# A hybrid decoder layer on one core: which engine makes four low parts of weights, the order of the state-space output, and where a query block is loaded

## The chip, the core and the metric

The kernel runs on one core of a Trainium2 chip. Its engines each run their own instructions in a fixed order: TensorE (PE in the profile) multiplies matrices, VectorE (DVE), ScalarE (ACT) and GpSimd (POOL) work elementwise, SyncE (SP) issues DMAs, and ScalarE and GpSimd issue some too. An instruction waits on its engine until what it reads is there and what it overwrites is free, and everything behind it on that engine waits as well. The metric is the time of one execution on the device, in microseconds (us). Three executions of the kernel before took 1641.96, 1643.04 and 1648.83 us; the median is 1643.04.

## The reference

The layer takes 512 tokens of width 1024 with 16 learned ones ahead, in float32. Two branches are merged by gates, and a mixer of experts follows.

```python
xn = rmsnorm(h, norm1_g[l])
proj = xn @ w_in[l]
u_s, x_m, z_m, g_s, g_m = jnp.split(proj, splits, axis=-1)     # 512, 1024, 1024, 1024, 1024 columns
y_s = s5_branch(u_s, ...) @ w_ssm_out[l]        # state-space scan, gelu, y * sigmoid(y @ w_glu + b_glu)
y_m = mlstm_branch(x_m, z_m, ...) @ w_ml_out[l] # causal convolution, 4 heads, matrix memory, gates
mixed = jax.nn.sigmoid(g_s) * y_s + jax.nn.sigmoid(g_m) * y_m
h = h + mixed @ w_out[l]
h = h + peer_ffn(rmsnorm(h, norm2_g[l]), peer_w_q[l], peer_sub_keys[l], peer_u[l], peer_v[l])
```

`peer_ffn` makes queries (`xb @ w_q`, 8 heads of 256 columns), picks 16 of 16384 experts per head by product keys, and sums the chosen rows of a table V, weighted by gates and by the gelu of products with rows of a table U.

## The kernel before

**Products in three parts.** A float32 product is made of three fast matmuls: each operand is cut into a high part (rounded to the type fp32r) and a low part (what the rounding left), and high x high, high x low and low x high are added up in one result buffer. In the profile these are L87, L90 and L91 (`mm3`) or L290, L292 and L293 (`proj`). `row3` is `mm3` with its matmuls kept in the order of the program; everywhere else a scheduler puts each engine's instructions in an order by its own estimates, before the kernel runs. `later(a, b)` adds a wait by hand: `a` comes after `b`.

**Blocks of weights.** `wblock` (L166) serves all weights of the front: a DMA on SP brings a block of 128 x 1024 into a raw buffer (`wraw`, two of them in turn), ScalarE copies it to the high part (L173, names ending in `_h`), and VectorE or GpSimd subtracts to make the low part (L176, recorded at L195, names ending in `_l`). High and low parts have two buffers each as well. `nblk` counts the blocks: 1 to 4 are those of u, then come wx0 (5), wgs0 (6), wx1 (7), wgs1 (8), wx2 (9), wgs2 (10) and so on, up to 24 for the second block of w_glu (`wglu2`), four blocks of w_ssm_out (25 to 28) and all later ones. L176 sends the low parts of blocks 2, 3, 6, 8 and of all from 29 on to GpSimd, the others to VectorE. The trace drops numbers from names: wx_l is the low part of any wx block.

**The stages that matter here.**
- *Projections.* PE multiplies xn (`xnh`, `xnl`) by the blocks of u, x (results `xm`, 264 columns at a time) and g_s (results `gs`). VectorE takes the results out (`xmt`, `mix`) and in the same time prepares the state-space scan: powers of the transition (`pw_r`, `pw_i`), and large products for its matrices (`w1r`, `w1i` and the helper `t`, in the listings `t3`, made from `s5p`; 128 x 2048 each). GpSimd does little besides.
- *State-space output* (L776 to L806). The scan's output `yg` is gated and split into `y2h` and `y2l`, four pieces (L775). Then y2 is multiplied by w_ssm_out: eight outputs so0 to so7, each of 4 x 3 matmuls of 512 columns, with two outputs to a block (wso0, wso2, wso4, wso6). Each sits in one of the four buffers of pool `mm` until VectorE multiplies it into `mix`. For the first two outputs the program writes piece 3 of y2 last.
- *Output and queries* (L1093 to L1150). `mixed` is multiplied by w_out in two passes over column halves, `c` = 0 and 1. In the second pass, for each of four tiles of 128 tokens, VectorE adds the output to x (`x0`, `x12`, `x3q`), ScalarE sums its squares (L1132), a chain of ten small VectorE steps takes the root (`n2e` is its first), L1142 scales, and PE transposes the result (`x2t`, L1108). Then the first two query blocks wq0 and wq1 are used; the other 14 follow in the expert stage.
- *Expert stage* (from about 450 us to the end): PE multiplies by the tables U (results `h`) and V (results `o`) block by block.

**Memory.** `half(name, slot)` names a tile in a fixed slot; a new tile of a slot waits until the old one has been read for the last time. Slot pB0 holds low parts of w_out in the first pass and later the tile `xn3`, of which only the half `xn3[:, 0]` is used (the scaled third tile).

Of the kernel before, what the change touches and what calls it, by code (L numbers as in the profile page):

```python
# [18 lines left out]
OP = mybir.AluOpType  # L19
# [4 lines left out]
P = 128  # L24
D = 1024
NK = D // P
# [36 lines left out]
def f32(ap):  # L63
    return ap.bitcast(F32)
# [68 lines left out]
def front(tc, a, dbg, cst, dram, xnp, ident, h2d, xsd, gds, x0, qt01, dump, split, mm3, rsqrt, rsqrt_cols):  # L133
    nc = tc.nc
    V, A, PE, GP, SY = nc.vector, nc.scalar, nc.tensor, nc.gpsimd, nc.sync
    es = ExitStack()
    with es:
# [7 lines left out]
        nblk = [0]  # L145
        NG = 20

        def half(name, slot, shape=(P, 4, T), dt=F32):

            pool = phase["pool"] if slot[0] == "p" else lng  # L150
            return pool.tile(list(shape), dt, tag=slot, name=name)
# [7 lines left out]
        highs, parts = [], {}  # L159
# [6 lines left out]
        def wblock(src, name, nk=NK, raw=None, on=None):  # L166

            if raw is None:
                raw = wload(src, name, nk)
            hi = wp.tile([P, NK, P], F32R, tag="whi", name=f"{name}_h")  # L170
            lo = wp.tile([P, NK, P], F32R, tag="wlo", name=f"{name}_l")
            nblk[0] += 1
            h_ = A.activation(hi[:, :nk], raw[:, :nk], AF.Copy)  # L173
            if on is not None:
                highs.append(later(h_, on))
            i_ = tt(lo[:, :nk], raw[:, :nk], f32(hi[:, :nk]), OP.subtract, GP if nblk[0] in (2, 3, 6, 8) or nblk[0] > NG + 8 else V)  # L176
            parts[name] = h_, i_
            if nblk[0] > NG + 22 and blank:
                blanks.append(later(SY.dma_start(blank.pop(0), zero.unsqueeze(1).to_broadcast([P, 2, D])), i_))
            return hi, lo  # L180

        def later(ins, on):

            tc.add_manual_dep(ins.ins, on.ins.name, mybir.DependencyInfo(
                mybir.DependencyClass.Sync, mybir.DependencyReason.SCHED_ONLY), reason="order")
            return ins
# [7 lines left out]
        def tt(o, x, y, op, eng=V):  # L194
            return eng.tensor_tensor(o, x, y, op=op)  # L195
# [180 lines left out]
        for j in range(L):  # L376
            for o, x in ((pv_r, pw_r), (pv_i, pw_i)):
                i_ = A.copy(o[:, :, j], x[:, :, L - 1 - j])
# [209 lines left out]
        for t_ in range(L):  # L588

            n = CH * (t_ + 1)  # L590
# [127 lines left out]
        def row3(ps_, lh, ll, rh, rl, first, last):  # L718
            row.matmul(ps_, lh, rh, start=first, stop=False)
            row.matmul(ps_, lh, rl, start=False, stop=False)  # L720
            return row.matmul(ps_, ll, rh, start=False, stop=last)
# [44 lines left out]
        for b in range(4):  # L766
            if b == 2:
                wb2 = wblock(a["w_glu"][b:b + 2].rearrange("b p k n -> p b k n"), f"wglu{b}")
            hi, lo = (x[:, b % 2 * 4:b % 2 * 4 + 4] for x in wb2)
            p = ptr(f"glu{b}")  # L770
            proj(hi, lo, p, lambda k: [ygh[:, k], ygl[:, k]], 4)
            sg = half(f"sglu{b}", ("pBr", "pBi")[b % 2], (P, S))
            A.activation(sg, p, AF.Sigmoid, bias=bglu[:, b:b + 1])
            tt(yg[:, b], yg[:, b], sg, OP.mult)
            lo_ = split(y2h[:, b], y2l[:, b], yg[:, b])  # L775
        dump("ys_glu", yg)  # L776
        sos = []

# [3 lines left out]

        for b in range(NK):
            if b % 2 == 0:
                wb2 = wblock(a["w_ssm_out"][b:b + 2].rearrange("b p k n -> p b k n"), f"wso{b}")
            hi, lo = (x[:, b % 2 * 4:b % 2 * 4 + 4] for x in wb2)
            p = pmm(f"so{b}", (P, L, NCR))
            sos.append((p, hi, lo, range(3) if b < 2 else range(4)))
            if b == 0:
                continue  # L790
            for p, hi, lo, ks in sos + [(*x[:3], (3,)) for x in sos if b == 1]:
                for k in ks:
                    mm3(p, hi[:, k], lo[:, k], y2h[:, k], y2l[:, k], k == 0, k == 3)
            done = [(n, sos[n][0]) for n in range(2)] if b == 1 else [(b, p)]
            sos = []
            for b_, p in done:
                opened_(b_, p)
# [6 lines left out]
        crs = half("crs", "pCi")[:H]  # L804
        for i in range(NT):
            cr = crs[:, i]  # L806
            V.tensor_scalar(dv[:, :i + 1], dv[:, :i + 1], fl[:, ST[i + 1] - 1:ST[i + 1]], None, op0=OP.add)
            V.tensor_scalar(cr[:, :NM], li[:, :NM], dv[:, 0:1], None, op0=OP.add)
            sh = [H, i + 1, P]
            tt(cr[:, NM:NM + (i + 1) * P].rearrange("h (j s) -> h j s", s=P),  # L810
               li[:, NM:NM + (i + 1) * P].rearrange("h (j s) -> h j s", s=P),
               dv[:, 1:i + 2].unsqueeze(2).to_broadcast(sh), OP.add)
            row.matmul(cbp[32 * i:32 * i + 32, 10], cr[:, :32], ident[:H, :H], start=True, stop=True)
            for j in range(i + 1):
                row.transpose(cbp[:, slot(j, i)], cr[:, NM + j * P:NM + (j + 1) * P], ident[:H, :H])
            row.transpose(cbp[:, 14 + i], em[:, NM + i * P:NM + (i + 1) * P], ident[:H, :H])
# [276 lines left out]
        for c, slots in ((0, ("pA1", "pB0", "mix0", "xmt0")), (1, ("xct0", "xct1", "pA0", "pB1"))):  # L1093
            wo = wout(c, slots)
            if c == 1:
                g2 = wp.tile([P, D], F32, tag="wraw", name="g2", bufs=2)
                A.dma_start(g2, a["g2"].to_broadcast([P, D]))
                xh = [xnp.tile([P, 4, S], F32R, tag="xn", name=f"x2h{j}") for j in range(2)]
                xl = [xnp.tile([P, 4, S], F32R, tag="xn", name=f"x2l{j}") for j in range(2)]
                wq = [wblock(a["w_q"][s_], f"wq{s_}") for s_ in range(2)]  # L1100
                qp = []
            def turned_(i, xn):

                first = None
                for j in range(2):
                    p = ptr(f"x2t{i}{j}", (P, 4, P))
                    for k in range(4):
                        i_ = PE.transpose(p[:, k], xn[:, (4 * j + k) * P:(4 * j + k + 1) * P], ident)  # L1108
                        if i > 1 and not first:
                            tc.keep_in_program_order(i_)  # L1110
                        first = first or i_
                    low[0] = split(xh[j][:, :, i * P:(i + 1) * P], xl[j][:, :, i * P:(i + 1) * P], p)

            def query(s_, n):

                t = slice(n * S // 2, (n + 1) * S // 2)
                if n == 0:
                    qp.append(pmm(f"q{s_}"))
                proj(*wq[s_], qp[s_][:, t], lambda k: [x[k // 4][:, k % 4, t] for x in (xh, xl)])
                A.copy(qt01[:, s_, t], qp[s_][:, t])  # L1120

            waiting = []
            for i in range(NT):
                p = pmm(f"wo{i}{c}")
                for k in range(NK):
                    lh, ll = (x[k // 4][:, k % 4, i * P:(i + 1) * P] for x in (mxh, mxl))
                    mm3(p, lh, ll, *wo[k], k == 0, k == NK - 1)
                cc = slice(c * 512, (c + 1) * 512)
                tt(xs[i][:, cc], p, xs[i][:, cc], OP.add)
                if c == 0:  # L1130
                    ss2.append(sm.tile([P, 2], F32, name=f"ss2{i}"))
                A.activation(sqj[:, cc], xs[i][:, cc], AF.Square, scale=1.0 / math.sqrt(D), accum_out=ss2[i][:, c:c + 1])  # L1132
                if c == 0:
                    continue
                A.dma_start(h2d[i * P:(i + 1) * P], xs[i])

                rstd = rsqrt_cols(sm, ss2[i][:, 0:1], 1, "n2", more=ss2[i][:, 1:2],
                                  pin=(lambda i_: later(i_, low[0])) if i == 2 else lambda i_: i_)
                if i == 1:
                    xn12, xn3 = half("xn12", "pA1", (P, 2, D)), half("xn3", "pB0", (P, 2, D))  # L1140
                xn = (xn12[:, 0], xn12[:, 1], xn3[:, 0])[i - 1] if i else x0
                V.scalar_tensor_tensor(xn, xs[i], rstd, g2, op0=OP.mult, op1=OP.mult)  # L1142
                if i == NT - 1:
                    A.dma_start(xsd, xn[P - MS:])
                waiting.append((i, xn))
                if i < 2:
                    turned_(*waiting.pop())
            if c:
                for s_ in range(2):
                    query(s_, 0)  # L1150
                    turned_(*waiting.pop(0))
                for s_ in range(2):
                    query(s_, 1)
# [800 lines left out]
```

## Time and profile before

| | us |
|---|---|
| median of three executions | 1643.04 |
| the profiled execution's own time | 1645.03 |
| its span, from the first to the last instruction | 1643.3 |
| busy: PE | 1612.1 |
| busy: VectorE | 1340.0 |
| busy: ScalarE | 727.8 |
| busy: GpSimd | 701.2 |

The mean granted clock of PE is 0.995 of full speed. In the timeline a row gives the start and the length of an instruction in us, its engine, line, operation and tiles, its shape, and in brackets how long the engine stood idle ahead of it and what ended that. Matmuls overlap: the step from start to start is what one costs PE, not its length. In a row of a window come the window's length, then busy time and number of instructions of PE, its weight loads, VectorE, ScalarE and GpSimd, then the granted clock, the busy share of the DMA engines and GB/s.

### The profile page before, as it was taken

The page shows a single profiled execution, that of the slowest core. Times are in us where ns is not written, and L with a number is a line of the kernel's source. Part 1 is how long each engine was busy: PE and PEld are TensorE (multiplying, and loading weights), DVE is VectorE, ACT ScalarE, POOL GpSimd, SP SyncE. Part 2 cuts the span into 40 slices and gives each one's busy share as a digit, 9 for nine tenths or more (in the row PEclk, how much of TensorE's full clock was granted, in tenths as well). Part 3 has the DMA queues.
Part 4 walks back from the last instruction along what each step waited for, and adds up shares of the span by engine and source line. Part 5 has one row for each costly group of instructions (what it writes and reads, how often), then busy time and mean ns, then how long its engine had stood idle before and what let it go on. Part 6 is the DMA issues. An engine that isn't in the chain of part 4 may idle for free. (4 is left out here: it accounts for less than half of the span.)

```text
span 1643.3 us, 25970 instructions
## 1 busy us (share of the span) xinstructions
PE 1612.1 (98%) x9671; PEld 1438.8 (88%) x9671; DVE 1340.0 (82%) x2675; ACT 727.8 (44%) x1202; POOL 701.2 (43%) x481
## 2 busy tenths in 40 slices
PE   9899999999999999999999999999999999999997
PEld 8798878888789899999999888888888888888886
DVE  6997556566578899999896498988988889898987
ACT  4454646733333244575664543334334333333334
POOL 3100023233122576877866244444444455555630
PEclk9999999999999999999999999999999999999999
DMA  4513322136463256889999899999999999999973
GB/s 170 117 53 95 112 81 73 60 106 216 153 221 99 74 138 175 271 294 344 304 363 319 325 373 393 385 373 367 399 372 399 357 398 382 371 401 366 389 282 139
DMA packets 148728, 423.48 MB, mean 258 GB/s; under 512 B 38485, under 2 KB 57557, under 8 KB 139129
## 3 DMA queue, kind: packets, MB, share of 16 engines
q1 hardware_dynamic: 87096, 263.52, 44.7%
q0 software_dynamic: 55360, 151.07, 26.0%
q10 hardware_dynamic: 6144, 7.23, 1.4%
q8 instruction: 76, 1.25, 0.3%
q14 instruction: 52, 0.42, 0.1%
HBM read 376.39 MB, written 45.38 MB: 257 GB/s over the span
## 5 line engine op out<-in xcount | busy, mean ns | idle before, releaser
L87 PE MATMUL h<-x2h,uh 128*128 128x352 f32 x1024 | 333.4, 326 | 1.5 <-ACT act L1239 0.9
L91 PE MATMUL h<-x2h,ul 128*128 128x352 f32 x1024 | 331.3, 324 | 3.0 <-DVE ul L84 2.9
L90 PE MATMUL h<-x2l,uh 128*128 128x352 f32 x1024 | 330.9, 323 | 0.0
L1276 POOL DMA_INDIRECT g<-in_v,e x128 | 187.6, 1466 | 160.3 <-DVE ac L1291 138.3
L87 PE MATMUL o<-vh,wh 128*128 128x512 f32 x768 | 240.5, 391 | 1.6 <-ACT wh L1820 1.6
L83 ACT ACTIVATE uh<-u 128x1024 fp32r<-128x1024 f32 x128 | 134.9, 1060 | 239.2 <-PE h L90 217.5
L90 PE MATMUL o<-vl,wh 128*128 128x512 f32 x768 | 240.0, 390 | 0.1
L1276 POOL DMA_INDIRECT g<-in_u,e x120 | 140.8, 1173 | 208.0 <-DVE g L1283 180.1
L91 PE MATMUL o<-vh,wl 128*128 128x512 f32 x768 | 224.0, 390 | 0.0
L1559 POOL DMA_INDIRECT gds<-cw,ix x96 | 189.3, 1972 | 57.0 <-DMA gds<-cw,ix 29.7
L87 PEld LDWEIGHTS h<-x2h,uh 128*128 128x128 f32 x1024 | 193.1, 189 | 6.8 <-ACT act L1239 2.5
L91 PEld LDWEIGHTS h<-x2h,ul 128*128 128x128 f32 x1024 | 192.4, 188 | 5.8 <-DVE ul L84 4.0
L90 PEld LDWEIGHTS h<-x2l,uh 128*128 128x128 f32 x1024 | 192.5, 188 | 1.8
L83 ACT ACTIVATE vh<-v 128x1024 fp32r<-128x1024 f32 x128 | 135.2, 1057 | 125.1 <-PE o L91 105.5
L84 DVE TENSOR_TENSOR vl<-v,vh 128x1024 fp32r<-128x1024 f32 x128 | 156.0, 1219 | 33.9 <-ACT vh L83 33.6
L84 DVE TENSOR_TENSOR ul<-u,uh 128x1024 fp32r<-128x1024 f32 x128 | 155.2, 1216 | 28.5 <-ACT uh L83 28.3
L91 PEld LDWEIGHTS o<-vh,wl 128*128 128x128 f32 x768 | 143.9, 188 | 30.3 <-DVE wl L1836 0.3
L90 PEld LDWEIGHTS o<-vl,wh 128*128 128x128 f32 x768 | 143.8, 188 | 29.4 <-DVE vl L84 0.4
L87 PEld LDWEIGHTS o<-vh,wh 128*128 128x128 f32 x768 | 143.2, 188 | 29.5 <-ACT wh L1820 2.3
L1291 DVE SCALAR_TENSOR_TENSOR ac<-g,w,ac 128x1024 f32<-128x1024 f32 x127 | 162.5, 1279 | 0.8
L1283 DVE SCALAR_TENSOR_TENSOR g<-g,x 128x1024 f32<-128x1024 f32 x120 | 144.5, 1216 | 0.0
L1820 ACT ACTIVATE wh<-w 128x384 fp32r<-128x384 f32 x128 | 66.9, 522 | 121.0 <-DVE w L1806 119.9
(579 smaller groups left out, 3125.4 us busy)
## 6 DMA issues: line engine op xcount, KB each, us to landing
u<-in_ut SPq DMA_DIRECT2D x64, 1024.0 KB, 7.7
v<-in_v SPq DMA_DIRECT2D x128, 512.0 KB, 9.0
gd<-stg SPq DMA_DIRECT2D x9, 2048.0 KB, 9.0
gi<-gd SPq DMA_DIRECT2D x16, 1152.0 KB, 16.1
ad<-act SPq DMA_DIRECT2D x38, 352.0 KB, 5.0
act<-ad SPq DMA_DIRECT2D x38, 352.0 KB, 11.4
wq<-in_w_q SPq DMA_DIRECT2D x14, 512.0 KB, 3.6
gds<-qt SPq DMA_DIRECT2D x6, 1024.0 KB, 5.3
```

The source lines that it names most:

```text
L83: pin(A.activation(hi, src, AF.Copy))
L84: return eng.tensor_tensor(lo, src, f32(hi), op=OP.subtract)
L87: i_ = PE.matmul(ps, lh, rh, start=first, stop=False)
L90: PE.matmul(ps, lh, rl, start=False, stop=False)
L91: return PE.matmul(ps, ll, rh, start=False, stop=last)
L1276: return GP.indirect_dma_start(out=t, out_offset=None, in_=a["u"] if s_ < P else a["v"], in_offset=bass.IndirectOffsetOnAxis(ap=e0[:, c:c ...
L1283: i_ = V.scalar_tensor_tensor(g, g, 1.0, x0, op0=OP.mult, op1=OP.mult, accum_out=hsl[:, c:c + 1])
L1291: i_ = V.scalar_tensor_tensor(ac0, g, w0[:, c:c + 1], ac0, op0=OP.mult, op1=OP.add)
L1559: i_ = GP.indirect_dma_start(out=gds.rearrange("i g b j t -> (i g b j t)").unsqueeze(1), out_offset=bass.IndirectOffsetOnAxis(ap=ix[:, c:c ...
L1820: tc.keep_in_program_order(A.activation(wh, w, AF.Copy))
```

## The change

```diff
@@ wblock
-            i_ = tt(lo[:, :nk], raw[:, :nk], f32(hi[:, :nk]), OP.subtract, GP if nblk[0] in (2, 3, 6, 8) or nblk[0] > NG + 8 else V)
+            i_ = tt(lo[:, :nk], raw[:, :nk], f32(hi[:, :nk]), OP.subtract, GP if nblk[0] in (2, 3) or nblk[0] > NG + 8 and name[:2] != "wq" else V)
@@ state-space output
-            lo_ = split(y2h[:, b], y2l[:, b], yg[:, b])
+            lo_ = split(y2h[:, b], y2l[:, b], yg[:, b], pin=halved.append)
...
-                wb2 = wblock(a["w_ssm_out"][b:b + 2].rearrange("b p k n -> p b k n"), f"wso{b}")
+                wb2 = wblock(a["w_ssm_out"][b:b + 2].rearrange("b p k n -> p b k n"), f"wso{b}",
+                             on=halved[-1] if b == 2 else None)
             hi, lo = (x[:, b % 2 * 4:b % 2 * 4 + 4] for x in wb2)
             p = pmm(f"so{b}", (P, L, NCR))
-            sos.append((p, hi, lo, range(3) if b < 2 else range(4)))
+            sos.append((p, hi, lo))
             if b == 0:
                 continue
-            for p, hi, lo, ks in sos + [(*x[:3], (3,)) for x in sos if b == 1]:
-                for k in ks:
-                    mm3(p, hi[:, k], lo[:, k], y2h[:, k], y2l[:, k], k == 0, k == 3)
+            for ks in ((0, 1), (2,), (3,)) if b == 1 else (range(4),):
+                for p, hi, lo in sos:
+                    for k in ks:
+                        row3(p, hi[:, k], lo[:, k], y2h[:, k], y2l[:, k], k == 0, k == 3)
...
-            V.tensor_scalar(dv[:, :i + 1], dv[:, :i + 1], fl[:, ST[i + 1] - 1:ST[i + 1]], None, op0=OP.add)
+            i_ = V.tensor_scalar(dv[:, :i + 1], dv[:, :i + 1], fl[:, ST[i + 1] - 1:ST[i + 1]], None, op0=OP.add)
+            if i == 0:
+                later(i_, parts["wso2"][1])
@@ queries
-                wq = [wblock(a["w_q"][s_], f"wq{s_}") for s_ in range(2)]
+                xn3 = half("xn3", "pB0", (P, 2, D))
+                raw = xn3[:, 1].rearrange("p (k n) -> p k n", k=NK)
+                SY.dma_start(raw, a["w_q"][1])
+                wq = [wblock(a["w_q"][s_], f"wq{s_}", raw=(None, raw)[s_]) for s_ in range(2)]
...
-                    xn12, xn3 = half("xn12", "pA1", (P, 2, D)), half("xn3", "pB0", (P, 2, D))
+                    xn12 = half("xn12", "pA1", (P, 2, D))
```

The low parts of wgs0 (block 6) and wgs1 (block 8), and of wq0 and wq1, go from GpSimd to VectorE. The matmuls of the state-space output go by `row3`: pieces 0 and 1 of y2 for so0 and so1, then piece 2, then piece 3, then each later output by itself. The high part of wso2 waits for the high part of y2's last piece, and the first step of the `crs` chain on VectorE waits for wso2's low part. The raw data of wq1 is loaded into the unused half `xn3[:, 1]`, so its DMA waits for slot pB0 and not for a `wraw` buffer.

The scheduler then orders the engines anew. In VectorE's order for the projections, around the low part of wx2 (numbers behind the names are the program's own), this stood before:

```order
L195 TENSOR_TENSOR w1r_581<-s5p_114 128x2048
L195 TENSOR_TENSOR xmt0_602<-xm11_732,nt_355 128x264
L195 TENSOR_TENSOR t3_585<-s5p_114 128x2048
L195 TENSOR_TENSOR w1i_582<-s5p_114 128x2048
L195 TENSOR_TENSOR wx2_l_931<-wx2_w_928,wx2_h_930 128x1024
L195 TENSOR_TENSOR w1r_581<-w1r_581,t3_585 128x2048
L195 TENSOR_TENSOR mix0_601<-gs1_815,nt_355 128x512
L195 TENSOR_TENSOR wgs2_l_992<-wgs2_w_989,wgs2_h_991 128x1024
```

and this stands there now:

```order
L195 TENSOR_TENSOR wx2_l_931<-wx2_w_928,wx2_h_930 128x1024
L195 TENSOR_TENSOR w1r_581<-s5p_114 128x2048
L195 TENSOR_TENSOR t3_585<-s5p_114 128x2048
L195 TENSOR_TENSOR w1i_582<-s5p_114 128x2048
L195 TENSOR_TENSOR mix0_601<-gs1_815,nt_355 128x512
L195 TENSOR_TENSOR wgs2_l_992<-wgs2_w_989,wgs2_h_991 128x1024
L195 TENSOR_TENSOR xmt0_602<-xm20_934,nt_355 128x264
L195 TENSOR_TENSOR w1r_581<-w1r_581,t3_585 128x2048
```

The low part of wx2 has moved ahead of three products of 128 x 2048, and the second step of w1r behind the low part of wgs2.

On PE, in the middle of the first four outputs of the state-space branch, the order before was:

```order
L87 MATMUL so0_2078<-y2h_1992,wso0_h_2074 128x512
L87 MATMUL so1_2079<-y2h_1992,wso0_h_2074 128x512
L87 MATMUL so2_2112<-y2h_1992,wso2_h_2108 128x512
L87 MATMUL so3_2126<-y2h_1992,wso2_h_2108 128x512
L90 MATMUL so0_2078<-y2l_1993,wso0_h_2074 128x512
L91 MATMUL so0_2078<-y2h_1992,wso0_l_2075 128x512
L90 MATMUL so1_2079<-y2l_1993,wso0_h_2074 128x512
L91 MATMUL so1_2079<-y2h_1992,wso0_l_2075 128x512
L90 MATMUL so2_2112<-y2l_1993,wso2_h_2108 128x512
L91 MATMUL so2_2112<-y2h_1992,wso2_l_2109 128x512
L90 MATMUL so3_2126<-y2l_1993,wso2_h_2108 128x512
L91 MATMUL so3_2126<-y2h_1992,wso2_l_2109 128x512
```

Now the last pieces of so0 and so1 stand by themselves, and so2 begins behind them:

```order
L711 MATMUL so0_2078<-y2h_1992,wso0_h_2074 128x512
L711 MATMUL so0_2078<-y2l_1993,wso0_h_2074 128x512
L711 MATMUL so0_2078<-y2h_1992,wso0_l_2075 128x512
L711 MATMUL so1_2079<-y2h_1992,wso0_h_2074 128x512
L711 MATMUL so1_2079<-y2l_1993,wso0_h_2074 128x512
L711 MATMUL so1_2079<-y2h_1992,wso0_l_2075 128x512
L711 MATMUL so2_2112<-y2h_1992,wso2_h_2108 128x512
L711 MATMUL so2_2112<-y2l_1993,wso2_h_2108 128x512
L711 MATMUL so2_2112<-y2h_1992,wso2_l_2109 128x512
```

Before, the four outputs end one right behind the other; now so0 and so1 end 24 matmuls ahead of so3 (the rows are recorded at L711, the helper of `row3`).

On ScalarE, at the end of the second output pass, the squares of token tiles 2, 3 and 0 (L1132) and the high parts of the query blocks stood like this:

```order
L1132 ACTIVATE x3q_4086,ss22_4193<-x12_4085 128x512
L173 ACTIVATE wq0_h_4251<-wq0_w_4249 128x1024
L1132 ACTIVATE x3q_4086,ss23_4221<-x3q_4086 128x512
L173 ACTIVATE wq1_h_4257<-wq1_w_4255 128x1024
L1132 ACTIVATE x3q_4086,ss20_4137<-x0_68 128x512
```

and now, with the square at L1139 of the changed file:

```order
L1139 ACTIVATE x3q_4086,ss22_4193<-x12_4085 128x512
L173 ACTIVATE wq0_h_4253<-wq0_w_4251 128x1024
L173 ACTIVATE wq1_h_4257<-xn3_4249 128x1024
L1139 ACTIVATE x3q_4086,ss23_4221<-x3q_4086 128x512
L1139 ACTIVATE x3q_4086,ss20_4137<-x0_68 128x512
```

The high part of wq1, read from xn3, has moved ahead of the square of the last tile of the first pass; the square of tile 0 in the second pass stays behind both.

## The prediction

> **What bounds the kernel now.** I read the engine shares first, then busy time by stretch, then what the matrix engine (PE) waits for.
>
> ```profile
> PE 1612.1 (98%) x9671; PEld 1438.8 (88%) x9671; DVE 1340.0 (82%) x2675; ACT 727.8 (44%) x1202; POOL 701.2 (43%) x481
> ...
> 40.00:153.40 113.40, 108.59 (x989) 101.06 (x989) 106.89 (x159) 53.80 (x95) 5.87 (x4) 0.98 0.32 80
> ...
> 1000.00:1200.00 200.00, 200.00 (x976) 174.08 (x975) 172.45 (x267) 74.98 (x133) 86.68 (x74) 1.00 1.00 383
> ...
> PE xm L293 <- DVE wx_l L195: 3.3, 2, 2.7
> PE x2t L1108 <- DVE x L1142: 2.2, 1, 2.2
> ...
> PE gs L87 <- ACT wgs_h L173: 0.9, 1, 0.9
> ```
>
> PE is the bound: it is idle for 31 us in all. In a stretch of the expert stage (1000 to 1200) it has no idle time at all. So a microsecond saved before that stage moves everything behind it, and the change can win only what PE loses in the three places it touches: the projections (40 to 153 us, where VectorE too is busy for 106.89 of 113.40 us), the state-space output (200 to 224) and the queries (around 440). The three wait rows (sum, times, longest) put 6.4 us there. That is not all, because a long wait also leaves PE at half clock:
>
> ```profile
> 54.36 0.39 PE L293 MATMUL xm<-xnh,wx_l 128*128 128x264 f32 x1 [0.68 <-DVE wx_l L195]
> ...
> 65.33 0.39 PE L290 MATMUL xm<-xnh,wx_h 128*128 128x264 f32 x1
> ...
> 66.99 0.50 PE L87 MATMUL gs<-xnh,wgs_h 128*128 128x512 f32 x1 [0.91 <-ACT wgs_h L173]
> ...
> 70.38 0.39 PE L293 MATMUL xm<-xnh,wx_l 128*128 128x264 f32 x1 [2.66 <-DVE wx_l L195]
> ...
> 70.87 0.42 PE L293 MATMUL xm<-xnh,wx_l 128*128 128x264 f32 x1
> ...
> 74.32 0.28 PE L290 MATMUL xm<-xnh,wx_h 128*128 128x264 f32 x1
> 74.44 0.29 PE L292 MATMUL xm<-xnl,wx_h 128*128 128x264 f32 x1
> ...
> 70.90:74.10 3.20, 3.20 (x16) 3.20 (x16) 3.20 (x3) 0.63 (x1) 0.00 (x0) 0.50 0.50 164
> ```
>
> Behind the 2.66 us wait the granted clock (the first number after the engines) is 0.50. From 70.87 to 74.32 sixteen matmuls start, 0.22 us apart; from 74.32 on they are 0.12 apart. That is 3.45 - 16 x 0.12 = 1.5 us lost after the wait. [...]
>
> **Part 1, the projections.** The change moves the low parts of the first two gate blocks (blocks 6 and 8) from GpSimd (POOL) to VectorE, and the scheduler then orders VectorE anew.
>
> ```profile
> 42.69 1.99 DVE L84 TENSOR_TENSOR wqkl<-wqk,wqkh 128x32 fp32r<-128x32 f32 x1
> ...
> 56.16 0.20 DVE L195 TENSOR_TENSOR ptmp<-pw_i,pw_r 128x32 f32<-128x32 f32 x1
> ...
> 57.67 1.82 DVE L195 TENSOR_TENSOR pw_i<-pw_i,ptmp 128x32 f32<-128x32 f32 x1
> ...
> 64.71 2.28 DVE L195 TENSOR_TENSOR t<-s5p 128x2048 f32<-128x2048 f32 x1
> ...
> 69.11 1.22 DVE L195 TENSOR_TENSOR wx_l<-wx_w,wx_h 128x1024 fp32r<-128x1024 f32 x1
> 70.24 2.28 DVE L195 TENSOR_TENSOR w1r<-w1r,t 128x2048 f32<-128x2048 f32 x1
> 72.45 0.68 DVE L195 TENSOR_TENSOR mix<-gs,nt 128x512 f32<-128x512 f32 x1
> ...
> 42.24 2.39 POOL L195 TENSOR_TENSOR wgs_l<-wgs_w,wgs_h 128x1024 fp32r<-128x1024 f32 x1 [3.71 <-ACT wgs_h L173]
> 57.03 2.41 POOL L195 TENSOR_TENSOR wgs_l<-wgs_w,wgs_h 128x1024 fp32r<-128x1024 f32 x1 [12.40 <-ACT wgs_h L173]
> ```
>
> Two tiny VectorE operations take 1.99 and 1.82 us, and both end within 0.1 us of a POOL operation's end (42.24 + 2.39 and 57.03 + 2.41). I take it that POOL held VectorE up. A row of their size takes 0.20 (56.16), so 1.8 + 1.6 = 3.4 us go. The two low parts come in at 1.13 us each (69.11 to 70.24, start to start), 2.3 in all. VectorE gains 1.1 us although it gets more work.
>
> The order matters more. Before, the low part of wx2 stands behind w1r, t and w1i, rows of 2.2 us each (64.71 to 69.11 for the last two), and ends at 70.24. After, it stands ahead of them. The same work, with both moved parts, ends at 70.24 - 1.1 = 69.1, so wx2's low part is ready at 69.1 - 6.6 = 62.5. PE, which starts on wx2 at 65.33, asks for it at about 65. So the 0.91 wait (a gate matmul that only stood there as a filler), the 2.66 wait and its 1.5 us of half clock go. The 0.68 wait goes too: the low part of wx1 ends some 1.3 us earlier, the 1.1 above less what is still to come from POOL's second operation, plus four short rows now behind it. Together **0.68 + 0.91 + 2.66 + 1.5 = 5.8 us**.
>
> What is late next? PE ends wx2's 48 matmuls at 65.33 - 0.68 + 48 x 0.12 = 70.4 and asks for the low part of the next gate block two gate matmuls of 0.227 (below) later, at 70.9. On VectorE it stands behind w1i and the product mix (0.68): 69.1 + 0.7 + 1.1 = 70.9. There is no margin. Later PE must not overtake VectorE:
>
> ```profile
> 152.65 0.71 DVE L195 TENSOR_TENSOR xct<-xct,qt 128x528 f32<-128x528 f32 x1 [0.71 <-ACT qt L493]
> ...
> 160.00 0.43 PE L647 MATMUL gate<-xct,wgt 128*32 128x264 f32 x4
> ...
> 153.61 4.60 ACTq L634 DMA_DIRECT2D yd<-ys  x4
> ```
>
> The gates need the last convolved block, which is 160.00 - 153.36 = 6.6 us early. After, PE is 5.8 earlier and VectorE 1.1, which leaves 1.9. The DMAs at 153.61 follow VectorE too, and so does what waits for them. For such places I take 0.8 us off: part 1 saves 5.0, with 1.0 (below) and 5.8 as ends.
>
> **Part 2, the state-space output.**
>
> ```profile
> 199.92 0.39 PE L87 MATMUL so<-y2h,wso_h 128*128 128x512 f32 x1
> ...
> 204.00 0.39 PE L87 MATMUL so<-y2h,wso_h 128*128 128x512 f32 x1
> ...
> 224.42 0.22 PE L711 MATMUL cbp<-ident,crs 4*32 4x4 f32 x2
> ...
> 204.31 0.63 ACT L83 ACTIVATE y2h<-yg 128x512 fp32r<-128x512 f32 x1 [1.69 <-DVE yg L195]
> ...
> 209.64 4.33 DVE L195 TENSOR_TENSOR mix<-so,mix 128x512 f32<-128x512 f32 x4 [2.90 <-PE so L91]
> ...
> 209.86 2.02 ACT L173 ACTIVATE wso_h<-wso_w 128x1024 fp32r<-128x1024 f32 x2 [4.92 <-PE so L90]
> ```
>
> 96 matmuls take 24.5 us. The first 18 start 0.227 apart (199.92 to 204.00); at that step all need 21.8. The 2.7 us come from an order in which the first four outputs all end together: then four products of VectorE (4.33 us) and two splits of weights come at once, and the next four outputs wait for result buffers and low parts. In the fixed order outputs 0 and 1 end after 24 matmuls, at about 205.4, and each product (1.1) has 12 matmuls, 2.7 us, beside it. The added wait holds the second block's split until the last y2 split is out (204.31 + 0.63 = 204.9 in before; earlier without that weight split ahead of it), and high and low part take 1.0 and 1.2 more, so both are ready within a microsecond of PE's asking, from 205.4 on. Behind it on ScalarE stand only the splits of blocks 4 and 6, which wait for PE anyway; the 4-row chain held behind it on VectorE is short and wanted at 221.8. **2.7 us**, with 1.5 (a low part 1.2 us late) as the low end.
>
> **Part 3, the queries.**
>
> ```profile
> 428.55 0.68 DVE L195 TENSOR_TENSOR x<-wo,x 128x512 f32<-128x512 f32 x1
> ...
> 428.66 7.42 SPq L163 DMA_DIRECT2D wq_w<-in_w_q  x2
> ...
> 440.92 1.90 DVE L110 SCALAR_TENSOR_TENSOR n2e<-ss 128x1 f32<-128x1 f32 x1 [6.23 <-ACT x3q L1132]
> ...
> 439.22 1.06 ACT L173 ACTIVATE wq_h<-wq_w 128x1024 fp32r<-128x1024 f32 x1 [5.41 <-DMA wq_w<-in_w_q]
> 440.41 2.40 POOL L195 TENSOR_TENSOR wq_l<-wq_w,wq_h 128x1024 fp32r<-128x1024 f32 x1 [4.69 <-ACT wq_h L173]
> ...
> 445.94 1.69 PE L1108 MATMUL x2t<-ident,x 128*128 128x128 f32 x8 [2.23 <-DVE x L1142]
> ...
> 453.08 1.03 PE L1108 MATMUL x2t<-ident,xn 128*128 128x128 f32 x8
> ...
> 446.40:449.50 3.10, 3.10 (x11) 2.68 (x10) 1.90 (x12) 1.69 (x4) 0.00 (x0) 0.50 0.42 169
> ```
>
> The sum of squares that the transposes need stood on ScalarE behind wq's second split, and that behind a DMA which waited for a raw buffer (the issue row of 7.42 us). With half of xn3 as its buffer that load goes out right behind the first. The second load of before took 3.1 (436.08 to 439.22); two in line land at 428.7 + 6.2 = 434.9, and the split ends at 436.0. VectorE does the low part (1.1) and x (0.7); then come the square (0.6, 440.28 to 440.92), n2e without POOL (0.2 as at 56.16, for 1.90) and the rest of the root and the scaling (3.1, from 442.82 to PE's start at 445.94). That makes 441.7. PE comes at 445.94 - 2.23 = 443.7, so 2 us of cover. The 2.23 wait goes, with its half clock: 1.69 - 1.03 on the transposes and 1.2 on six output matmuls in the 0.50 window. **4.1 us**; low end 0.
>
> **Sum.** 5.0 + 2.7 + 4.1 = 11.8, say 12. The profiled execution took 1645.03, so 1633.0 there; it stands 2.0 over the median of 1643.04, which gives **1631.0**.
>
> **Rivals.**
> - *VectorE stays the bound of the projections.* For it: 106.89 of 113.40 us busy. [...] In rows: if the 1.99 and 1.82 were no hold-up, VectorE is 3.4 later, PE waits 3.3 for the next gate block and loses 1.5 to the clock. Part 1 then saves about 1.0, all three 7.8: 1635.2. Against it: both long rows end where POOL's do.
> - *The second query load doesn't go out early*, because its half tile shares slot pB0 with weights of the first output pass. Part 3 saves nothing: 1635.1. Against: those weights are read for the last time ahead of the 428.55 row, which adds that pass's last output.
> - *The gain is swallowed later*, DMA being busy for 1.00 of 1000 to 1200: 1643. Against: PE waits for no DMA there.
> - *Slower: moved pieces in the expert stage.* The new order shifts a dozen blocks among PE's later matmuls by up to some 80 places. A piece that now comes before its low part costs a wait and the half clock, 2.23 + 1.9 = 4.1 us as above. From the third such place the gain is gone; five cost 20.5 and give 1651.5. Against: in most of that stage PE waits for nothing.
>
> **How the numbers follow.** Forecast 0.62, with a range of its own from 1628 to 1634; VectorE the bound 0.15; load not early 0.08; swallowed 0.10; slower 0.05. The range 1627 to 1638 takes in the first three, which is 0.85, less some for error. A measurement of this kernel can tell about 0.5% (8.2 us) from no change: faster means under 1634.8. That is the forecast and a third of the next two, about 0.68; slower 0.04; the rest the same.
>
> **What would show it.** Right: no half-clock window near 71 and 446; VectorE's longest 128x32 rows about 0.2; so's 96 matmuls in under 22.3 us; ScalarE's second wq split ending near 436 on this time scale less about 8. Wrong: a wait of over 2 us for a gate block's low part near 71, a transposes' wait still there, or PE idle beyond 700 us grown by as much as the front has saved.

## The result, and the profile after

| | before | changed |
|---|---|---|
| median of the first six runs each, us | 1644.02 | 1636.26 |
| lowest and highest | 1641.96 to 1648.83 | 1634.53 to 1637.24 |
| the profiled execution's own time | 1645.03 | 1634.53 |
| its span | 1643.3 | 1632.4 |

The ratio is 0.9949, with a 95% interval from 0.9934 to 0.9963; nine further runs of the changed kernel gave 0.9957 (0.9943 to 0.9970). The change saves 7.8 us, where 12 were forecast. That is 0.5%, small but clear of the noise, as both intervals end below 1. The forecast of 1631.0 is missed by 5.3 us: 4.2 are the smaller saving, 1.0 the median of before, which is 1644.02 in six runs where three had given 1643.04.

First the line of busy times of the changed kernel, then its two longest waits of PE between 40 and 160 us (sum, times, longest).

```profile
PE 1608.0 (99%) x9671; PEld 1438.1 (88%) x9671; DVE 1338.6 (82%) x2679; ACT 726.6 (45%) x1202; POOL 702.0 (43%) x477
...
PE xm L290 <- DVE mix L195: 2.2, 1, 2.2
PE gs L91 <- DVE wgs_l L195: 0.6, 1, 0.6
```

The waits that were forecast to go have gone: those for wx_l, wgs_h, so and x2t are no longer in the list. In their place stands one of 2.2 us on VectorE's product `mix`. The timeline of VectorE and ScalarE shows how it came:

```profile
42.89 0.18 DVE L84 TENSOR_TENSOR wqkl<-wqk,wqkh 128x32 fp32r<-128x32 f32 x1
...
59.76 0.19 DVE L195 TENSOR_TENSOR pw_i<-pw_i,ptmp 128x32 f32<-128x32 f32 x1
...
62.56 1.23 DVE L195 TENSOR_TENSOR wx_l<-wx_w,wx_h 128x1024 fp32r<-128x1024 f32 x1 [0.47 <-ACT wx_h L173]
65.82 2.29 DVE L195 TENSOR_TENSOR w1r<-s5p 128x2048 f32<-128x2048 f32 x1 [2.04 <-ACT s5p L378]
68.03 2.28 DVE L195 TENSOR_TENSOR t<-s5p 128x2048 f32<-128x2048 f32 x1
70.23 2.29 DVE L195 TENSOR_TENSOR w1i<-s5p 128x2048 f32<-128x2048 f32 x1
72.43 0.69 DVE L195 TENSOR_TENSOR mix<-gs,nt 128x512 f32<-128x512 f32 x1
73.03 1.22 DVE L195 TENSOR_TENSOR wgs_l<-wgs_w,wgs_h 128x1024 fp32r<-128x1024 f32 x1
...
61.47 1.06 ACT L173 ACTIVATE wx_h<-wx_w 128x1024 fp32r<-128x1024 f32 x1 [0.51 <-DMA wx_w<-in_w_in]
62.43 0.34 ACT L378 COPY s5p<-pw_i 128x16 f32<-128x16 f32 x2
62.67 0.83 ACT L484 ACTIVATE xct<-xmt,par 128x528 f32<-128x528 f32 x1
63.50 1.28 ACT L537 ACT_TABLE_LOAD   x1
64.80 0.63 ACT L537 ACTIVATE mix<-mix 128x512 f32<-128x512 f32 x1
65.33 0.46 ACT L378 COPY s5p<-pw_r 128x16 f32<-128x16 f32 x3
```

The two VectorE operations that took 1.99 and 1.82 us now take 0.18 and 0.19: GpSimd did hold them up (a later run puts two such operations back and shows the hold-up again). The low part of wx2 ends at 63.79, in time. But then VectorE stands idle for 2.04 us, until ScalarE's copies of the powers (`s5p`, L378) are made, and these stand behind a table load of 1.28 and the first gate's sigmoid of 0.63. `w1r`, `t`, `w1i`, the product of gate 1 and the low part of wgs2 follow one another without a gap, all late by that. PE's rows and three windows (engines as before, then the granted clock):

```profile
73.27 0.36 PE L290 MATMUL xm<-xnh,wx_h 128*128 128x264 f32 x1 [2.21 <-DVE mix L195]
...
74.31 0.55 PE L91 MATMUL gs<-xnh,wgs_l 128*128 128x512 f32 x1 [0.56 <-DVE wgs_l L195]
74.65 0.63 PE L87 MATMUL gs<-xnh,wgs_h 128*128 128x512 f32 x1
...
78.06 0.40 PE L91 MATMUL gs<-xnh,wgs_l 128*128 128x512 f32 x1
...
74.70:78.00 3.30, 3.30 (x9) 2.63 (x8) 3.30 (x3) 0.83 (x1) 0.00 (x0) 0.50 0.54 156
431.00:440.00 9.00, 9.00 (x45) 7.55 (x44) 6.64 (x25) 2.08 (x7) 0.00 (x0) 1.00 0.29 117
1000.00:1200.00 200.00, 200.00 (x978) 174.24 (x977) 171.33 (x264) 76.42 (x135) 85.70 (x74) 1.00 0.99 378
```

PE loses 2.21 + 0.56 us, and then eight matmuls take 3.41 us (74.65 to 78.06) where 8 x 0.227 = 1.8 would do: 1.6 more at half clock. Around the transposes (431 to 440) PE is busy throughout at full clock.

For the other two parts, the first rows are PE's at the start and behind the end of the 96 matmuls of the state-space output (219.81 - 197.96 = 21.85 us), the last two ScalarE's split of the second query block and the first step of the root:

```profile
197.96 0.39 PE L711 MATMUL so<-y2h,wso_h 128*128 128x512 f32 x1
...
219.81 0.22 PE L711 MATMUL cbp<-ident,crs 4*32 4x4 f32 x2
...
428.62 1.06 ACT L173 ACTIVATE wq_h<-xn 128x1024 fp32r<-128x1024 f32 x1 [0.18 <-DMA xn<-in_w_q]
...
432.88 0.16 DVE L110 SCALAR_TENSOR_TENSOR n2e<-ss 128x1 f32<-128x1 f32 x1 [0.79 <-ACT x3q L1139]
```

The split ends at 429.68. The end of the state-space output came 4.6 us earlier than before, so this is 434.3 on the scale of the profile before, where 436 had been forecast; and the root's first step takes 0.16 us where it took 1.90.

Executions differ by some 3 us in when the first xm matmul starts (39.39 to 42.77), so stages are measured within one trace: **P** from the first xm matmul to the first gate matmul, **S** from the first so matmul to the first cbp matmul, **Q** from there to the first matmul of the key scores (`sc`), **E** from the first gather matmul (`gp`) to the last matmul of the expert stage. For the kernel before P is 160.00 - 40.92, S is 224.42 - 199.92. The runs are told of below; each was set against runs of the kernel before on the same chip.

| kernel | P | S | Q | E | median (runs) |
|---|---|---|---|---|---|
| before | 119.08 | 24.50 | 246.79 | 955.57 | 1644.02 (6) |
| before, second profile | 119.65 | 24.54 | 245.25 | 954.39 | |
| changed | 116.85 | 21.85 | 242.64 | 953.34 | 1636.26 (6) |
| changed, second profile | 117.33 | 21.86 | 242.71 | 954.69 | 1636.24 (9) |
| part 1 alone | 117.02 | 24.54 | 246.74 | 956.15 | 1639.53 (10) |
| part 2 alone | 119.23 | 21.85 | 244.77 | 954.03 | 1640.91 (10) |
| part 3 alone | 119.12 | 24.53 | 242.71 | 954.71 | 1642.24 (10) |
| copies first | 113.56 | 21.85 | 242.71 | 957.82 | 1634.49 (6) |
| copies and low part first | 112.30 | 21.86 | 242.74 | 957.86 | 1633.90 (6) |
| the same, second profile | 112.37 | 21.86 | 242.70 | 954.60 | 1634.07 (6) |

### The profile page after: what moved, and what is told of

Read it like the earlier page. It is cut to its first block, busy times and chain, and to the rows that moved or that the text cites. A ratio compares the mean times of both kernels' runs of the same rounds, so it can differ in the third digit from the quotient of the medians.

```text
span 1632.4 us, 25970 instructions
## 1 busy us (share of the span) xinstructions
PE 1608.0 (99%) x9671; PEld 1438.1 (88%) x9671; DVE 1338.6 (82%) x2679; ACT 726.6 (45%) x1202; POOL 702.0 (43%) x477
## 4 chain that ended last, share of the span: by engine, by line
PE 85%; DVE 8%; DMA 3%; ACT 2%; issue 1%; POOL 0%; ACTq 0%; SPq 0%; DVEq 0%
PE o L87 10%; PE o L90 10%; PE o L91 10%; PE h L91 9%; PE h L87 9%; PE h L90 8%; PE gm L711 3%; PE z L711 2%; PE gp L1646 2%; PE so L711 1%; PE q L90 1%; PE q L87 1%; PE q L91 1%; PE n L711 1%; PE wo L87 1%
## 5 line engine op out<-in xcount | busy, mean ns | idle before, releaser
L1283 POOL DMA_INDIRECT g<-in_v,e x128 | 197.9, 1546 | 149.3 <-DVE ac L1298 124.8
L87 PE MATMUL o<-vh,wh 128*128 128x512 f32 x768 | 244.9, 391 | 1.5 <-ACT wh L1827 1.5
L90 PE MATMUL o<-vl,wh 128*128 128x512 f32 x768 | 244.3, 390 | 0.1
```

The costliest lines, as they stand in the source:

```text
L87: i_ = PE.matmul(ps, lh, rh, start=first, stop=False)
L90: PE.matmul(ps, lh, rl, start=False, stop=False)
L1283: return GP.indirect_dma_start(out=t, out_offset=None, in_=a["u"] if s_ < P else a["v"], in_offset=bass.IndirectOffsetOnAxis(ap=e0[:, c:c ...
```

## The experiments

**The changed kernel again, and each part alone.** No edit for the first; the other three take one part of the diff and leave the other two out.

> The changed kernel once more, as a measure of what two profiles of one kernel differ by. Theory (the 2.2 us that the changed kernel's profile gains behind 650 us, at a wait of 1.64 us at 798 that shrank to 0.35 and at short gate matmuls at 910, are a matter of one execution): the waits of the front come again within 0.1 us (2.2 near 73, the gates at 158.0, the cb matmuls at 219.8, the last query matmul at 454.9), but the wait near 788 is over 1 us again, and the span is about 1633.5 to 1635. Rival (they come from the new order of matmuls in the expert stage): the wait near 788 stays under 0.5 us and the span stays within 0.5 us of 1632.4.

> The change's first part alone: the low parts of the first two gate blocks on VectorE, all else as before. Theory (the three parts are independent; this one wins only 2.2 of the 5.0 us that were forecast, since a wait of 2.2 us and a stretch at half clock come back near 73): the gate matmuls that began at 160.00 begin at 158.0, the state-space output takes 24.5 us as before, the transposes still wait 2.2 us, and the time is 2.2 us below that of before. Rival (the new wait near 73 comes from the other two parts' orders): no wait of over 1 us near 73, and the gates at about 155.5.

> The change's second part alone: the state-space output in fixed order with its two waits, low parts and queries as before. Theory (independent parts): the front up to 199.92 as before, the 96 matmuls in 21.8 us, the matmuls behind them 2.65 us earlier than before, and that is kept to the end of the front: time 2.7 us below before. Rival (the earlier y2 splits and waits shift work of the projections too): the gates move from 160.00 by more than 0.3 us.

> The change's third part alone: the second query block loaded into half of xn3, both low parts of queries on VectorE. Theory (independent parts): nothing moves up to 440; the transposes' wait of 2.2 us and the half clock behind it go, and the last query matmul of the front comes 4.1 us earlier; time 4.1 us below before. Rival (the expert stage gives part of it back, since its DMAs are the bound there): 4.1 us earlier at 465, less than 3 at 1600.

The stages answer in the table. Part 1 moves P alone, from 119.1 to 117.0, with the new wait in it; part 2 moves S alone among P and S, by 2.65; part 3 alone brings Q to 242.71, 4.1 less than in the first profile of before. So the parts are independent, and the new wait belongs to part 1. In ratios, part 1 has 0.9975 (0.9963 to 0.9988), part 2 0.9982 (0.9968 to 0.9995), part 3 0.9992 (0.9980 to 1.0005): 4.1, 3.0 and 1.3 us of 1643.68. The first is more than P gives, the last less than Q gives, and its interval takes in no change at all. Single executions of one kernel lie 3 to 8 us apart, and a part's worth is read from its stage, not from these.

One surprise stands in Q: part 2 alone has 244.77, though it leaves the queries as they were. The changed kernel's second profile decides on the expert stage: E is 954.69 where it was 953.34, with a wait of 1.7 us near 788 that was 0.2 in the first. So most of the 2.2 us that the first profile gained there were a matter of that execution, though its span of 1632.7 is nearer to what the rival had named; the second profile of before, with 954.39, shows none of them.

**The kernel before, a second profile.**

> The kernel before once more, for a second profile. Theory (the waits come from the order and recur in every execution, the half clock behind them does not: behind the wait of 24.5 it came in three of five profiles so far): waits of 2.66 near 70 and 2.2 near 446 again, within 0.5 us; stretches at half clock behind them may be missing, and where one is missing the time behind it is 1.5 to 1.9 us less. Rival (the half clock follows from the wait's length): a half-clock stretch of over 3 us behind both waits again, as in the first profile.

This is one execution, of 1644.80 us. The wait near 70 recurred to the hundredth, 2.66, with half clock behind it (0.50 in the first window below). At the transposes the wait was 1.69, and the clock stayed at 1.00:

```profile
72.23 0.59 PE L293 MATMUL xm<-xnh,wx_l 128*128 128x264 f32 x1 [2.66 <-DVE wx_l L195]
...
447.90 1.09 PE L1108 MATMUL x2t<-ident,x 128*128 128x128 f32 x8 [1.69 <-DVE x L1142]
...
72.40:75.80 3.40, 3.40 (x16) 3.40 (x17) 3.40 (x3) 0.63 (x1) 0.00 (x0) 0.50 0.51 154
...
448.10:450.10 2.00, 2.00 (x14) 1.78 (x13) 1.01 (x6) 1.56 (x4) 0.00 (x0) 1.00 0.36 145
```

So Q of the old queries is 246.79, 245.25, 246.74 and 244.77 in four profiles, 245.9 in the mean, and with part 3 it is 242.7 every time. Part 3 is worth 3.2 us in the mean: some 4.1 in the two profiles where the clock drops behind the transposes (246.79 and 246.74, with 0.81 over 441 to 450 in both), and 2.3 in the mean of the two where it doesn't (1.00).

**Copies ahead of the sigmoid.** Three of ScalarE's copies of each kind are kept, and the first gate's sigmoid waits for them.

```diff
+        copied = []
         for j in range(L):
             for o, x in ((pv_r, pw_r), (pv_i, pw_i)):
                 i_ = A.copy(o[:, :, j], x[:, :, L - 1 - j])
                 if j == L - 1:
                     later(i_, xhs)
+                elif j < 3:
+                    copied.append(i_)
...
                 opened.append(later(A.activation(o, o, AF.Sigmoid), sine))
+                if b == 0:
+                    for x in copied:
+                        later(opened[-1], x)
```

> The changed kernel, with one order more: ScalarE's copies of the last three powers (s5p from pw_r and pw_i) come ahead of the table load and the first gate's sigmoid. Theory (the new wait near 73 comes from ScalarE: VectorE stood idle for 2.04 us until 65.82, because those copies were queued behind the table load of 1.28 and the sigmoid of 0.63): w1r begins near 63.9, the product of gate 1 and the low part of wgs2 are ready 2 us earlier, PE waits under 1.2 us in all between 70 and 75 instead of 2.77, and the gates that began at 158.04 begin between 154.5 and 156.2; time 2 to 3.5 us below the changed kernel's median of 1636.24, 1632.7 to 1634.2. Rival (VectorE's sheer work bounds the projections): w1r begins earlier, but PE's waits come back between 75 and 155, the gates begin at 158.04 less at most 0.5, and the time stays within 0.5 us of 1636.2.

VectorE's and PE's rows of this kernel, where the executions' start is 1.6 us earlier than in the profile above:

```profile
62.39 2.29 DVE L195 TENSOR_TENSOR w1r<-s5p 128x2048 f32<-128x2048 f32 x1
...
70.23 0.39 PE L290 MATMUL xm<-xnh,wx_h 128*128 128x264 f32 x1 [0.56 <-ACT wx_h L173]
```

`w1r` has no wait in front of it any more, PE's wait is 0.56, the next xm matmul takes 0.28 us, where such a matmul took 0.42 at half clock in the prediction's rows, and P falls by 3.3 to 3.8 us, to 113.56. The rival, VectorE's sheer work as the bound, would have left P at 116.3 or more. ScalarE's order was the cause. The median of 1634.49 (0.9937, 0.9916 to 0.9958) is 1.8 us below the changed kernel, a little short of the 2 that were expected, with E at 957.82. The intervals of the two kernels overlap, here and for the orders below: the gain is shown by the stage, not by the median.

**Copies and low part first.** In addition the product `w1i` waits for the product of gate 1 and the low part of wgs2.

```diff
-            outer(gsgate(b)) if not b else gsgate(b)
+            gs1 = outer(gsgate(b)) if not b else gsgate(b)
...
-        outer(gsgate(2))
+        gs2 = gsgate(2)
+        later(outed[3], parts["wgs2"][1])
+        later(outed[3], gs1)
+        outer(gs2)
```

Here `outed` collects the instructions that `outer` issues.

> As the run before, and the product w1i (2.3 us) also waits for the product of gate 1 and the low part of wgs2, so that these two stand ahead of it on VectorE. Theory (order, not work, makes PE wait): no wait of PE over 0.5 us between 70 and 80 and no half clock there, the gates begin near 153.5, 4.5 us ahead of the changed kernel; time 1631.7. Rival (VectorE's work is the bound): w1i and what follows it come 1.8 us later, PE waits for transposes of w1i or for a later low part, and the gates begin no earlier than 156.

PE waits nowhere between 60 and 150 us now, and P is 112.30, 4.55 less than in the changed kernel: the forecast was 4.5. Against the first profile of before P is 6.8 us shorter, more than the 5.8 that the prediction took for the most that part 1 could give. Of the gain 0.7 us are lost again right behind P (1.5 in the second profile), where PE waits for the parts of a gate block. Behind the front the gain meets the expert stage, with E at 957.86, and the median stands at 1633.90, only 2.3 below the changed kernel (0.9935, 0.9918 to 0.9953). One place shows how. VectorE, PE and a window of this kernel, then VectorE of the changed one:

```profile
1012.60 0.52 DVE L1823 TENSOR_TENSOR w<-gi,act 128x352 f32<-128x352 f32 x1 [7.48 <-DMA gi<-gds]
...
1013.79 0.74 PE L87 MATMUL o<-vh,wh 128*128 128x512 f32 x2 [2.49 <-ACT wh L1837]
...
1015.00:1018.41 3.41, 3.41 (x11) 2.73 (x10) 3.41 (x7) 1.00 (x4) 1.99 (x2) 0.50 1.06 369
```

```profile
1012.75 0.53 DVE L1813 TENSOR_TENSOR w<-gi,act 128x352 f32<-128x352 f32 x1 [3.96 <-DMA gi<-gds]
```

PE came there some 5 us earlier (its first expert output matmul starts at 922.42 instead of 927.85), but the gathered weights (`gi`) landed at the same time, and PE waited 2.49 us that it had not waited before, with 3.41 us at half clock behind it, half of which, 1.7, is lost as well. So the same kernel was profiled again:

> The kernel with the copies and the low part first, once more. Theory (the front's 4 us are kept up to the expert stage in every execution, and that stage takes 953 to 958 us in ten profiles whatever the front does): waits of the front within 0.2 us of the first profile; from the first gather matmul to the last output matmul 953 to 958 us; median of 1632 to 1634.5, 2 to 4 us below the changed kernel. Rival (the expert stage's gathers set a floor in time, so an earlier front only waits longer there): the wait for a weight near 1014 is over 2 us again, the stage takes over 957 us again, and the median is 1634 or more.

E was 954.60 this time, without that wait, and the median 1634.07 (0.9943, 0.9927 to 0.9959), which suits both. The theory's range for E held and the rival's recurrence failed; yet E was 957.8, 957.9, 954.6 and 958.9 in the four profiles with the earliest fronts, against 953.3 to 958.2 in ten others. The granted clock sorts them better than the front does. Five of the fourteen profiles have one stretch at half clock in the expert stage (near 786, 1015, 932, 790 and 1018 us), and there E is 956.5 to 958.9; in the nine without one it is 953.3 to 956.2. Three of them, by windows: 0.52 over 786.60 to 789.60 (copies first), 0.50 over 1015.00 to 1018.41 above, and 0.69 over 790 to 795 (the late load, below). Ahead of the stretch stands, in two of the four profiles with early fronts, a wait for the gathers' weights (2.49 us, and 2.15 in the last run below), in one a wait for another block (2.02); the other two are of kernels whose front is as late as the changed one's. So an early front can lose its gain at the gathers; that it must, as with a floor, is not shown.

**Low parts of the queries on GpSimd.**

```diff
-            i_ = tt(lo[:, :nk], raw[:, :nk], f32(hi[:, :nk]), OP.subtract, GP if nblk[0] in (2, 3) or nblk[0] > NG + 8 and name[:2] != "wq" else V)
+            i_ = tt(lo[:, :nk], raw[:, :nk], f32(hi[:, :nk]), OP.subtract, GP if nblk[0] in (2, 3) or nblk[0] > NG + 8 else V)
```

> The changed kernel with the low parts of the two query blocks back on GpSimd; the early load into xn3 stays. Theory (the early load does most of part 3, and VectorE's part is that GpSimd no longer holds up small steps of VectorE): ScalarE's second wq split ends as early as in the changed kernel, GpSimd's two low parts take 2.4 us each and end before the root's small steps begin or hold one of them for about 1.7 us; PE waits for the transposes for less than 0.8 us, and the front ends within 1 us of the changed kernel. Rival (the low parts on VectorE are what counts): the transposes wait over 1.5 us again and the last x2t comes over 2 us later.

Q is 242.73 as in the changed kernel, with no wait for the transposes; the single execution took 1639.80 us, with E at 958.24. Yet the hold-up is there, word for word in the rows of VectorE and GpSimd:

```profile
431.19 2.40 DVE L110 SCALAR_TENSOR_TENSOR n2e<-ss 128x1 f32<-128x1 f32 x1 [0.79 <-ACT x3q L1139]
...
431.18 2.40 POOL L195 TENSOR_TENSOR wq_l<-xn,wq_h 128x1024 fp32r<-128x1024 f32 x1
```

A step of 0.16 us (in the changed kernel) takes exactly as long as GpSimd's operation beside it. The early load gives enough cover to hide it, in this one profile.

**Late load of the second query block.** The lines on `xn3` and `raw` are undone; the low parts stay on VectorE.

> The changed kernel with the second query block loaded into its old raw buffer; both low parts of queries stay on VectorE. Theory (the early load is what part 3 lives by; the run with the low parts on GpSimd kept all of it): the second load waits for the first low part again, which VectorE makes in 1.2 us instead of GpSimd's 2.4, so it comes only some 1 to 2 us earlier than before; the square and the root follow it, and PE waits 0.5 to 2 us for the transposes, the front ending 0.5 to 4 us later than in the changed kernel. Rival (either half of the part is enough): no wait of PE over 0.3 us there and the front within 0.3 us of the changed kernel.

The transposes wait 0.56 us, and Q is 244.14, 1.5 above the changed kernel (one execution, 1637.82 us). So, by one profile of each, the early load alone gives the whole of part 3, and the move to VectorE adds nothing beside it. By itself the move gives less: Q is 0.9 us below the mean of the two profiles of the old queries without half clock there (245.25 and 244.77), where the early load gives 2.3. But the wait that is left is short, 0.56 us against the 1.69 of before's second profile.

**Fixed order without the two waits.**

```diff
-            lo_ = split(y2h[:, b], y2l[:, b], yg[:, b], pin=halved.append)
+            lo_ = split(y2h[:, b], y2l[:, b], yg[:, b])
...
-                             on=halved[-1] if b == 2 else None)
...
-            if i == 0:
-                later(i_, parts["wso2"][1])
```

> The changed kernel without the two added waits of the state-space output: the matmuls stay in fixed order, but the second weight block's split no longer waits for the last y2 split, and the crs chain not for its low part. Theory (the fixed order spreads the outputs' ends, and the waits are needed to have y2's last piece in time): that weight block and the chain stand ahead of the last y2 piece on ScalarE and VectorE again, its low part comes about 5.8 us behind the first output matmul instead of 3.9, PE wants it 4.1 behind, so PE waits 1.5 to 2 us there, and the 96 matmuls take 23.4 to 24 us, or up to 1.5 more if the clock drops behind the wait. Rival (the order of matmuls alone does it): 96 matmuls in under 22.3 us.

```profile
203.25 0.50 PE L711 MATMUL so<-y2h,wso_h 128*128 128x512 f32 x1 [0.84 <-ACT y2h L83]
...
204.05 0.50 PE L711 MATMUL so<-y2l,wso_h 128*128 128x512 f32 x1 [0.29 <-DVE y2l L84]
```

S is 23.54 (one execution, 1637.78 us): PE waits 0.84 and 0.29 us for the last piece of y2, and the steps around bring it to 1.7. For the low part of the second weight block, where the wait was expected, PE doesn't wait. The fixed order alone gives 1.0 of the 2.65, the waits the rest.

**The split ahead of ScalarE's DMA issues**, on top of copies and low part first:

```diff
-            (SY, A)[t_ % 2].dma_start(yd[t_].rearrange("g c n -> c g n"), ys[t_ * CH:(t_ + 1) * CH])
+            later((SY, A)[t_ % 2].dma_start(yd[t_].rearrange("g c n -> c g n"), ys[t_ * CH:(t_ + 1) * CH]), parts["wgs6"][0])
```

> The kernel with copies and low part first, and the eight DMAs of the scan's output (yd from ys, four of them issued by ScalarE in 4.6 us) wait for the high part of the seventh gate block, so that this split stands ahead of them on ScalarE. Theory (what took back 0.7 and 1.5 us of the gain at the gates is ScalarE, which issues those DMAs while PE wants that block): the two waits of PE near 157 and 159 (0.5 each) go, the first state-space output matmul comes 112.3 + 39.9 = 152.2 us behind the first xm matmul instead of 152.9 and 153.7, and the time is 0.7 to 1.5 us below 1634.0. Rival (the DMAs then come late themselves): the scan's output comes 1 us later or more, ScalarE's split of the first z block or the gelu wait for it, PE waits at the z or glu matmuls, and the first output matmul comes no earlier than 153.

The two waits went, but PE then waits 0.9 us at a z matmul for VectorE's `mix`, and the first output matmul stands 153.36 us behind the first xm matmul, between the 152.90 and 153.74 of the two profiles without this edit. The median is 1635.17 (0.9943, 0.9930 to 0.9957). Nothing is won. The rival's number holds, and so does its place, the z matmuls; but what PE waits for there is VectorE's `mix`, not ScalarE's split.

## Why the prediction was right in part

- **Part 1 is where it failed**: 2.1 us (P) against 5.0. The step is "the same work, with both moved parts, ends at 70.24 - 1.1 = 69.1". It took VectorE for busy throughout and summed only its own rows. Its chain ended at 72.43: VectorE waited 0.47 us for the high part of wx2 and 2.04 for ScalarE's copies, because ScalarE's order had changed too: before, three copies of the last six stood ahead of the table load, after, all six behind it. ScalarE before:

```profile
61.55 0.47 ACT L378 COPY s5p<-pw_r 128x16 f32<-128x16 f32 x3
62.03 1.28 ACT L537 ACT_TABLE_LOAD   x1
...
63.87 0.45 ACT L378 COPY s5p<-pw_i 128x16 f32<-128x16 f32 x3
```

  The prediction read VectorE's order and not ScalarE's. "There is no margin" was said of the very place where PE then waited; the value taken should have been nearer the low end of 1.0. Of its signs of being wrong one came: PE waited 2.21 us near 73, though for the product `mix` and only 0.56 more for the gate block's low part, and a window at half clock (0.50) followed.
- **GpSimd's hold-up** was right: 1.99 and 1.82 became 0.18 and 0.19. The rival "VectorE stays the bound", whose 1635.2 lies nearest to the 1636.26, rested on its denial and fell: the nearest number belongs to a mechanism that was not at work. VectorE's work is not the bound: with two orders changed, P falls to 112.3 with no work removed.
- **Part 2** was right in kind and size: 2.65 against 2.7. The added waits are needed for it.
- **Part 3** was right in its mechanism, and of 4.1 in the profile that it was worked out from. Its mean over four profiles of the old queries is 3.2, since the wait and the half clock behind it vary from one execution to the next. The term was taken from one execution as if it held for all.
- **The sum** then is 2.1 + 2.65 + 3.2 = 8.0, against 7.8 measured and 11.8 forecast; 2.9 of the 3.8 that were too much are part 1's. The result lies in the range of 1627 to 1638 by that range's breadth, which also covered two rivals, and not by the working; it lies outside the 1628 to 1634 given to the forecast's own mechanism, and above the 1634.8 below which the prediction expected the time with a chance of about 0.68. No place in the expert stage took anything back that the two profiles of each kernel show alike (E 955.57 and 954.39 before, 953.34 and 954.69 after), so neither the rival of moved pieces nor that of a swallowed gain came in.

## What to carry to other kernels

When a change lets a scheduler order one engine anew, read the new order of every engine that this one waits for: what a sum over one engine's rows promises ends at the first thing that it waits for from another. A copy of some 0.12 us (three in 0.36 above, from start to start) is worth placing ahead of a table load (1.28) if a chain of 2 us products hangs on it. And size a gain at a stall from several profiles of the same kernel, since the wait itself and the clock behind it differ between them (at the transposes 2.23 us with 0.50 behind it in one profile of before, 1.69 with 1.00 in the other).

## What the runs showed of the hardware

The half clock doesn't follow from a wait's length alone. At one place of the expert stage a wait of 2.41 us was followed by full clock in one kernel, and one of 2.27 by half clock in another; the windows give 1.00 and 0.69 for the 5 to 6 us behind:

```profile
790.63 0.43 PE L91 MATMUL h<-x2h,ul 128*128 128x352 f32 x1 [2.41 <-DVE ul L84]
...
790.00:796.00 6.00, 5.37 (x33) 5.37 (x34) 6.00 (x6) 1.41 (x2) 5.09 (x4) 1.00 0.59 177
```

```profile
790.11 0.66 PE L91 MATMUL h<-x2h,ul 128*128 128x352 f32 x1 [2.27 <-DVE ul L84]
...
790.00:795.00 5.00, 4.89 (x22) 4.89 (x23) 5.00 (x6) 0.00 (x0) 4.39 (x3) 0.69 0.68 166
```

The first is the run with the queries' low parts on GpSimd, the second that with the late load. What sets the two apart is not shown.

Half clock also followed waits of 2.66 and 2.23 us in the first profile of before, 2.21 in the changed kernel (with 0.56 more right behind it), and 2.49 with copies and low part first. In the first profile of before it lasted from 70.81 to 74.22 and from 446.27 to 449.68, 3.41 us each; in the changed kernel from 74.62 to 78.03, 3.41 as well.

Far shorter waits differ in this too: one of 0.79 us at 24.4 was followed by half clock in the first profile of before (0.83 over 20 to 30), and one of 0.81 in the second profile of the changed kernel was not (1.00).

GpSimd's hold on a VectorE operation lasted to the end of GpSimd's own: 431.19 + 2.40 and 431.18 + 2.40 above.
